# Copying the cache pages to DRAM ahead of time, and handing three kinds of low-part subtraction to GpSimd

## The chip, the cores and the metric

One NeuronCore of one Trainium2 chip runs the whole program. The metric is the device time of one execution in microseconds (us). A core has five engines with in-order instruction streams: TensorE (PE), VectorE (DVE), ScalarE (ACT), GpSimd (POOL) and SyncE (SP), which here issues nearly all DMAs.

## The reference

One inference step of a two-layer decoder trunk in float32, for one prompt of 1024 tokens and 8 sample rows of one token each, 1024 wide. Layer 0 is a Mamba-2 branch and a Conformer branch side by side. Layer 1 is sparse attention, and all that the change touches computes this:

```python
q, k, v, qi, ki, wi, z = odd_project(x, w_in)
scores = sum_h relu(qi_h . ki_all) * wi_h          # 8 index heads of 64
_, idx = lax.top_k(scores, 256)                    # per query
p = softmax(q . k_sel / 8)                         # 16 heads, 4 key heads
o = p . v_sel
y = layer_norm(ALPHA * x + (o * silu(z)) @ w_out)
```

For the 8 sample rows, keys, values and index keys of the past are read from paged caches: 8 rows times 8 pages of 128 positions, found through `page_table`. Prompt and sample rows share all weights.

## The kernel before

**Products in split float32.** A weight or activation is split into a high part (rounded to fp32r by a cast) and a low part (the difference), and a product is three matmuls, high x high, high x low, low x high (`mm3`, L132 to L134). `load_w` loads a 128x1024 block of weights in two halves of 128x512, casts each to its high part on ACT (L108) and subtracts to get the low part (L109) on DVE or POOL, by its argument `eng`. A projection block is one `load_w` and three column chunks (0, 344, 688) of 24 matmuls each.

**Layer 0** (about 0 to 937 us of the span) is a row of such blocks for the Conformer gate and values (GLU), the Mamba inputs, the gates and the output, with convolutions and recurrences on DVE and ACT beside them.

**Layer 1** has four parts that overlap.

- Index projections and index scores S (L970 to L977) and, for the sample rows, index keys read from the pages by 64 DMAs (`fetch`, L869; the page's number is loaded into a register of SP and used in the DMA's address), then scores Ss (L1006, L1024).
- Projections of queries (`QQ`, 8 blocks, L1045), keys (`KK`, 2 blocks) and gates (`ZZ`, 8 blocks). A query chunk leaves PSUM by a cast on ACT (L1051) and a subtraction from PSUM on DVE (L1052), and both parts go to DRAM. Sample keys are read from the pages by 64 more `fetch` DMAs and multiplied with the sample queries (L1104).
- The top-k of every row, a bitwise search for the threshold. Four blocks of query rows are searched together on DVE (search `d`, L1175: one counting pass per block and bit; 16 bits on the upper half word, 16 on the lower). Two blocks (search `a`) and the sample rows (search `s`) are searched by sign counts on ACT (L1164, tiles `jka` and `jks`), with three small DVE instructions per bit (L1166, L1148, L1150). Then masks are made on DVE (L1217 to L1245).
- Attention, 8 query tiles of 8 steps: logits (L1314), mask and maximum on DVE (L1315, L1318), exponentials on ACT (L1319), transposes (L1341), weighted values (L1350), and, between steps, the output product (L1402) and sample work, among it `sample_values`, which reads values by 64 `fetch` DMAs.

Python generators and a scheduler write the final order of each engine before the launch; at run time each engine goes through its own list in order and waits on semaphores. A tile tag with one buffer forces its uses into one sequence: a new tile of the tag comes after all uses of the tile before it. `jk` + name (L1163) gives each search a scratch tile of its own.

Of the kernel before, what the change touches and what calls it, by code (L numbers as in the profile page):

```python
# [124 lines left out]
def mm3(k, out, w, act, t0, n, m=128, halves=2, start=True, stop=True):  # L125

    nc = k.nc
    for kt in range(8):
# [5 lines left out]
        nc.tensor.matmul(out, wl, ah, start=False, stop=(stop and kt == 7))  # L134
# [42 lines left out]
def layer0(k):  # L177
# [232 lines left out]
    def xbc(i, dest):  # L410
# [290 lines left out]
    def out_b(m):  # L701
        w = load_w(k, A["W"][OB + m], eng=nc.gpsimd)
        for t0, n in CH:
# [114 lines left out]
def layer1(k):  # L818
# [35 lines left out]
    def ev(dt=F32):  # L854
        return k.t(tk, [128, 344], dt, "ev", 3)


    pgr = k.t(right, [1, 64], I32, "pgr")
    nc.sync.dma_start(pgr, A["pt"])

    def numbers(b, j, n):

        o = b * 8 + j
        return nc.values_load_multi_w_load_instructions(
            pgr[0:1, o : o + n], engines=[mybir.EngineType.SP],
            skip_runtime_bounds_check_because="a page table holds numbers of pages of the pool")[1]

    def fetch(dst, src, v, rows=128):
        nc.sync.dma_start(dst, src[bass.ds(v * rows, rows), :])  # L869
# [189 lines left out]
    for i in range(2):  # L1059
        w = load_w(k, A["W"][KK + i])  # L1060
# [57 lines left out]
    for i in range(8):  # L1118
        w = load_w(k, A["W"][ZZ + i])
# [13 lines left out]
    def search(name, R_, cols, count, above, last):  # L1133
# [582 lines left out]
```

## Time and profile before

| | us |
|---|---|
| median of 3 runs | 1729.22 (1726.86 to 1737.44) |
| profiled execution | 1731.68 |
| its span | 1729.9 |
| PE busy | 1607.1 (93%) |
| DVE busy | 1205.6 (70%) |
| ACT busy | 898.6 (52%) |
| POOL busy | 243.1 (14%) |

The profiled execution is 2.5 us above the median. The span leaves 1.8 us around it. Busy shares are means over the whole span; the stages have different limits, so the view by stretches is the one to read.

### The profile page before, as it was taken

The page shows a single profiled execution, that of the slowest core. Times are in us where ns is not written, and L with a number is a line of the kernel's source. Part 1 is how long each engine was busy: PE and PEld are TensorE (multiplying, and loading weights), DVE is VectorE, ACT ScalarE, POOL GpSimd, SP SyncE. Part 2 cuts the span into 40 slices and gives each one's busy share as a digit, 9 for nine tenths or more (in the row PEclk, how much of TensorE's full clock was granted, in tenths as well). Part 3 has the DMA queues.
Part 4 walks back from the last instruction along what each step waited for, and adds up shares of the span by engine and source line. Part 5 has one row for each costly group of instructions (what it writes and reads, how often), then busy time and mean ns, then how long its engine had stood idle before and what let it go on. Part 6 is the DMA issues. An engine that isn't in the chain of part 4 may idle for free.

```text
span 1729.9 us, 28861 instructions
## 1 busy us (share of the span) xinstructions
PE 1607.1 (93%) x10334; PEld 1443.8 (83%) x10334; DVE 1205.6 (70%) x2742; ACT 898.6 (52%) x2142; POOL 243.1 (14%) x280
## 2 busy tenths in 40 slices
PE   8988989998999998997998999598899899999996
PEld 7988989998999997996898998488889567676674
DVE  4778887426466878757665468999996766565673
ACT  5467464354345464535334455465752765555663
POOL 4000000001212234122322200000000411112120
PEclk9999999999999999998999999698999999999998
DMA  6222242246111145433421212242344723543460
GB/s 220 81 89 59 80 101 87 91 136 239 40 42 63 63 154 194 128 116 117 145 69 53 85 54 77 76 141 94 95 147 136 226 46 99 141 107 86 97 138 32
DMA packets 164497, 183.65 MB, mean 106 GB/s; under 512 B 20194, under 2 KB 131130, under 8 KB 164098
## 3 DMA queue, kind: packets, MB, share of 16 engines
q1 hardware_dynamic: 161842, 176.05, 34.2%
q0 software_dynamic: 1216, 4.37, 0.7%
q8 instruction: 81, 1.33, 0.3%
q10 hardware_dynamic: 1296, 1.38, 0.2%
q14 instruction: 62, 0.51, 0.1%
HBM read 129.81 MB, written 51.95 MB: 105 GB/s over the span
## 4 chain that ended last, share of the span: by engine, by line
PE 70%; DVE 20%; issue 3%; DMA 3%; ACT 2%; POOL 2%; DVEq 0%; ACTq 0%; POOLq 0%; SPq 0%
PE pp L132 12%; PE pp L134 12%; PE pp L133 12%; DVE jkd L1175 6%; PE po L1402 5%; PE pv L1350 4%; PE lg L1314 4%; PE tr L1341 4%; DVE uv L333 3%; PE pt L600 2%; PE pt L134 1%; PE pt L133 1%; PE pt L132 1%; PE pt L574 1%; PE po L1407 1%
## 5 line engine op out<-in xcount | busy, mean ns | idle before, releaser
L132 PE MATMUL pp<-act,whi 128*128 128x344 f32 x1088 | 353.7, 327 | 20.9 <-DVE uv L296 11.1
L134 PE MATMUL pp<-act,wlo 128*128 128x344 f32 x1088 | 354.6, 327 | 4.9 <-DVE wlo L109 4.9
L133 PE MATMUL pp<-act,whi 128*128 128x344 f32 x1088 | 353.5, 325 | 0.7 <-POOL act L699 0.7
L132 PEld LDWEIGHTS pp<-act,whi 128*128 128x128 f32 x1088 | 207.9, 192 | 24.7 <-DVE uv L296 11.6
L134 PEld LDWEIGHTS pp<-act,wlo 128*128 128x128 f32 x1088 | 208.1, 192 | 6.8 <-DVE wlo L109 5.1
L133 PEld LDWEIGHTS pp<-act,whi 128*128 128x128 f32 x1088 | 207.9, 191 | 3.1 <-issue 1.0
L108 ACT CAST whi<-wst 128x512 fp32r<-128x512 f32 x148 | 90.8, 618 | 146.2 <-PE pp L133 72.6
L333 DVE SCALAR_TENSOR_TENSOR uv<-uv,cst,uv 128x1024 f32<-128x1024 f32 x120 | 157.3, 1311 | 2.9
L132 PE MATMUL pp<-yh,whi 128*128 128x344 f32 x408 | 136.4, 334 | 16.4 <-DVE ev L1052 9.9
L109 DVE TENSOR_TENSOR wlo<-wst,whi 128x512 fp32r<-128x512 f32 x104 | 71.2, 690 | 106.5 <-ACT whi L108 106.4
L134 PE MATMUL pp<-yh,wlo 128*128 128x344 f32 x408 | 134.7, 330 | 3.3 <-DVE wlo L109 2.4
L1315 DVE CUSTOM_DVE_ANT_0 P<-lg,w 128x512 f32<-128x512 f32 (+3 forms) x144 | 83.0, 598 | 59.9 <-PE lg L1314 53.7
L348 ACT ACTIVATE cft<-cw,own 128x40 f32<-128x40 f32 x512 | 113.9, 313 | 13.2 <-DMA cw<-dct 8.6
L1314 PE MATMUL lg<-w,Q 128*128 128x512 f32 (+3 forms) x384 | 103.2, 372 | 2.3 <-DVE nmx L1315 2.0
L132 PEld LDWEIGHTS pp<-yh,whi 128*128 128x128 f32 x408 | 80.2, 197 | 21.2 <-DVE ev L1052 11.3
L1341 PE MATMUL tr<-cst,P 128*128 128x128 f32 x576 | 84.4, 279 | 3.2 <-ACT P L1319 2.1
L1341 PEld LDWEIGHTS tr<-cst,P 128*128 128x128 f32 x576 | 64.2, 141 | 26.2 <-issue 14.7
L1319 ACT ACTIVATE P<-P,mx 128x1024 f32<-128x1024 f32 (+3 forms) x64 | 63.3, 989 | 43.3 <-DVE mx L1318 42.7
L1350 PE MATMUL pv<-ph,V 128*64 128x256 f32 (+1 forms) x640 | 82.1, 372 | 2.4 <-DVE ph L1344 1.6
L134 PEld LDWEIGHTS pp<-yh,wlo 128*128 128x128 f32 x408 | 80.1, 196 | 4.7 <-DVE wlo L109 3.9
L109 POOL TENSOR_TENSOR wlo<-wst,whi 128x512 fp32r<-128x512 f32 x44 | 57.9, 1319 | 154.9 <-ACT whi L108 143.9
L1314 PEld LDWEIGHTS lg<-w,Q 128*128 128x128 f32 x384 | 62.5, 191 | 20.6 <-DVE nmx L1315 8.4
(567 smaller groups left out, 3850.8 us busy)
## 6 DMA issues: line engine op xcount, KB each, us to landing
wst<-in_W SPq DMA_DIRECT2D x148, 256.0 KB, 2.8
Q<-dq SPq DMA_DIRECT2D x64, 256.0 KB, 4.1
dq<-ev SPq DMA_DIRECT2D x48, 172.0 KB, 1.8
q<-in_ck SPq DMA_DIRECT2D x64, 128.0 KB, 2.4
vp<-in_cv SPq DMA_DIRECT2D x64, 128.0 KB, 2.2
xst<-in_xT SPq DMA_DIRECT2D x8, 516.0 KB, 9.0
dzb<-ob SPq DMA_DIRECT2D x24, 172.0 KB, 2.0
uv<-dzb SPq DMA_DIRECT2D x8, 516.0 KB, 5.0
```

Source lines behind the costliest of these rows:

```text
L108: nc.scalar.copy(hi, st)
L109: (eng or nc.vector).tensor_tensor(lo, st, hi.bitcast(F32), op=ALU.subtract)
L132: nc.tensor.matmul(out, wh, ah, start=(start and kt == 0), stop=False)
L133: nc.tensor.matmul(out, wh, al, start=False, stop=False)
L134: nc.tensor.matmul(out, wl, ah, start=False, stop=(stop and kt == 7))
L333: nc.vector.scalar_tensor_tensor(out, x, w[:, j : j + 1], y, op0=ALU.mult, op1=ALU.add)
L348: nc.scalar.activation(wv[:, :, ch, :], cw[:, g, : NBT - 1].rearrange("q (d p) -> q d p", p=PH), AF.Copy, scale=own[:, ch : ch + 1])
L1175: nc.vector.tensor_scalar(jk, col, c, 0.0, op0=op, op1=ALU.add, accum_out=cnt)
L1314: mm = nc.tensor.matmul(lg, Q[:, 4 * a + r, :], KT[g][:, s0 : s0 + m], start=(a == 0), stop=(a == 1))
L1341: nc.tensor.transpose(p[:, a, r * 128 : r * 128 + 128], Ps[r][:, (sb + a) * 128 : (sb + a) * 128 + 128], k.ident)
L1350: nc.tensor.matmul(pv[64 * u : 64 * u + 64, 256 * pr + c0 : 256 * pr + c1], V[:, sb + a, g * 64 : g * 64 + 64], ph[:, a, c0:c1], start=(sb ...
L1402: nc.tensor.matmul(p, a[:, kt, :], W[kt][w][:, sl], start=start and n == 0, stop=stop and n == 2, skip_group_check=True)
```

## The change

It does six things.

1. At the start of layer 0 it creates three DRAM buffers and copies all 192 cache pages into them in an order that later needs no page numbers (`four_pages`, four pages a call). Each call is written behind the middle column chunk of a projection block and wrapped in `tc.issue_after(mm)`. The later reads become plain DMAs: 8 for the index keys, 16 of 512 KB for the sample keys, 32 for the values.
2. A query chunk is read from PSUM twice by ACT (`hi` and `full`), and POOL makes `lo` from two SBUF tiles. The pool `ev` has 5 buffers, not 3.
3. The low parts of the query, key and gate weights (36 instructions of 128x512) go to POOL.
4. In search `d` one small DVE instruction per bit is folded into its neighbour.
5. Searches `a` and `s` share one scratch tile `jk` with one buffer.
6. The value tiles are pairs (`vp`, 6 buffers of two pages).

```diff
+    def four_pages(after):
+        if not todo:
+            return
+        what, b, hf = todo.pop(0)
+        with tc.issue_after(after):
+            o = b * 8 + 4 * hf
+            _, vs = nc.values_load_multi_w_load_instructions(
+                pgr[0:1, o : o + 4], engines=[mybir.EngineType.SP], ...)
+            for j, v in enumerate(vs, 4 * hf):
+                if what == "ckidx":
+                    nc.sync.dma_start(k.dki[j, b // 2, 64 * (b % 2) : 64 * (b % 2) + 64], A[what][bass.ds(v * 64, 64), :])
+                else:
+                    nc.sync.dma_start((k.dck if what == "ck" else k.dcv)[b, j], A[what][bass.ds(v * 128, 128), :])
...
-            mm3(k, p, w, x, t0, n)
+            mm = mm3(k, p, w, x, t0, n)
+            if t0 == 344:
+                four_pages(mm)
...
-        for b in range(NS):
-            for j, v in enumerate(numbers(b, 4 * hf, 4)):
-                fetch(kg[j // 2][64 * (b % 2) : 64 * (b % 2) + 64, j % 2, b // 2, :], A["ckidx"], v, 64)
+        for j in range(4):
+            nc.sync.dma_start(kg[j // 2][:, j % 2], k.dki[4 * hf + j].rearrange("r p x -> p r x"))
...
-        w = load_w(k, A["W"][QQ + i])
+        w = load_w(k, A["W"][QQ + i], eng=nc.gpsimd)
...
-            hi, lo = ev(F32R), ev(F32R)
+            hi, full = ev(F32R), ev()
             nc.scalar.copy(hi, p)
-            nc.vector.tensor_tensor(lo, p, hi.bitcast(F32), op=ALU.subtract)
+            nc.scalar.copy(full, p)
+            lo = ev(F32R)
+            nc.gpsimd.tensor_tensor(lo, full, hi.bitcast(F32), op=ALU.subtract)
...
+            flip = 1 << (bit - 1) if bit > last else 0
+            if bit < 31 and placed:
+                nc.vector.scalar_tensor_tensor(new, no, flip, cand, op0=ALU.bitwise_xor, op1=ALU.bitwise_xor)
...
-            jk = k.t(sc_pool, [128, 1032], BF16, "jk" + name, 1)[:rows, :w]
+            jk = k.t(sc_pool, [128, 1032], BF16, "jk", 1)[:rows, :w]
```

Where instructions stand now. On SP, in the first microseconds of layer 0, the order before was this (`wst` are weights, `xst` the input):

```order
L231 DMA xst_164<-in_xT 128x1032
L231 DMA xst_170<-in_xT 128x1032
L105 DMA wst_299<-in_W 128x512
L105 DMA wst_305<-in_W 128x512
L105 DMA wst_400<-in_W 128x512
L247 DMA dct_88<-taps_177 128x8x328
L105 DMA wst_406<-in_W 128x512
```

and in the changed kernel the same place reads (`pgr` is the page table, `dki` the index keys' buffer):

```order
L261 DMA xst_171<-in_xT 128x1032
L261 DMA xst_177<-in_xT 128x1032
L215 TENSOR_LOAD pgr_97
L220 ISA
L220 DMA dki_94<-in_ckidx 16x512
L220 ISA
L220 DMA dki_94<-in_ckidx 16x512
L220 ISA
L220 DMA dki_94<-in_ckidx 16x512
L220 ISA
L220 DMA dki_94<-in_ckidx 16x512
L105 DMA wst_319<-in_W 128x512
```

All 192 copies stand in this manner between the weight loads of the first seven GLU blocks; the last is SP's 487th row of 1057, just ahead of the first weights of the eighth block:

```order
L222 DMA dcv_15_96<-in_cv 16x2048
L222 ISA
L222 DMA dcv_15_96<-in_cv 16x2048
L105 DMA wst_2413<-in_W 128x512
```

On DVE, at the first attention instruction (L1315 before, L1350 now), the order before ended the sample rows' masks and a weight's low part first:

```order
L1241 TENSOR_SCALAR eq_14141<-Ss_9967,nxts_14135 8x1025
L1242 SCALAR_TENSOR_TENSOR cum_14142<-eq_14141 8x1025
L1243 SCALAR_TENSOR_TENSOR eq_14141<-cum_14142,needs_14139,eq_14141 8x1025
L1244 TENSOR_SCALAR cum_14142<-Ss_9967,nxts_14135 8x1025
L1245 TENSOR_TENSOR Ss_9967<-cum_14142,eq_14141 8x1025
L109 TENSOR_TENSOR wlo_12836<-wst_12833,whi_12835 128x512
L1315 ISA P_14194,nmx_14192<-lg_14195,w_12968 128x512
```

and now it is preceded by rounds of search `s` (`nos`, `cands`), 13 of them between the last mask of search `a` (the L1280 row) and the first L1350:

```order
L1280 TENSOR_TENSOR w_13254<-cum_14391,eq_14390 128x512
L1198 TENSOR_TENSOR nos_14119<-cnts_14118,lims_14066 8x1
L1180 SCALAR_TENSOR_TENSOR cands_14123<-nos_14119,cands_14115 8x1
...
L1198 TENSOR_TENSOR nos_14215<-cnts_14214,lims_14066 8x1
L1180 SCALAR_TENSOR_TENSOR cands_14219<-nos_14215,cands_14211 8x1
...
L1350 ISA P_14465,nmx_14463<-lg_14466,w_13253 128x512
L1350 ISA nmx_14463 128x1
```

Of the 32 rounds, 6 stand ahead of the end of search `a`'s masks, 13 here, and 13 between the attention steps of the first query tiles; the sample masks follow in steps 10 to 12, and the first output product follows 140 logit matmuls, where it followed 80 before. A piece of POOL's list now reads as follows in the last query blocks and the gates' weights; before, none of these rows stood on POOL:

```order
L109 TENSOR_TENSOR wlo_12195<-wst_12192,whi_12194 128x512
L1081 TENSOR_TENSOR ev_12074<-ev_12071,ev_12070 128x344
L109 TENSOR_TENSOR wlo_12201<-wst_12198,whi_12200 128x512
L109 TENSOR_TENSOR wlo_12341<-wst_12338,whi_12340 128x512
L109 TENSOR_TENSOR wlo_12347<-wst_12344,whi_12346 128x512
```

POOL keeps only these subtractions between the index scores and the first attention outputs.

## Rows read from the trace of the kernel before

**Rows 1.** The page's busy times, and its 40 slices of the span (one digit is the busy share in tenths).

```profile
PE 1607.1 (93%) x10334; PEld 1443.8 (83%) x10334; DVE 1205.6 (70%) x2742; ACT 898.6 (52%) x2142; POOL 243.1 (14%) x280
PE   8988989998999998997998999598899899999996
DVE  4778887426466878757665468999996766565673
PEclk9999999999999999998999999698999999999998
```

**Rows 2.** Busy time of each engine by stretch: start and end, length, then busy us (count) of PE, PEld, DVE, ACT, POOL, then the granted clock, DMA share and GB/s.

```profile
1060.00:1100.00 40.00, 32.69 (x170) 27.85 (x168) 38.35 (x101) 18.55 (x41) 0.84 (x2) 0.83 0.18 50
1100.00:1140.00 40.00, 24.89 (x120) 21.37 (x120) 38.95 (x123) 18.98 (x44) 0.00 (x0) 0.74 0.42 126
1140.00:1180.00 40.00, 33.34 (x175) 31.85 (x176) 39.56 (x131) 22.79 (x51) 0.00 (x0) 0.84 0.37 116
1180.00:1220.00 40.00, 37.12 (x221) 36.55 (x221) 39.34 (x136) 29.73 (x65) 0.00 (x0) 0.94 0.30 95
1220.00:1260.00 40.00, 35.07 (x251) 32.56 (x250) 39.28 (x133) 31.18 (x68) 0.00 (x0) 0.96 0.35 103
1260.00:1290.00 30.00, 26.51 (x214) 24.83 (x213) 29.56 (x87) 17.85 (x40) 0.00 (x0) 1.00 0.42 131
1290.00:1340.00 50.00, 49.89 (x408) 46.81 (x406) 36.43 (x65) 13.19 (x25) 0.00 (x0) 1.00 0.49 150
1340.00:1400.00 60.00, 54.59 (x345) 34.68 (x345) 46.18 (x122) 44.19 (x70) 23.25 (x14) 1.00 0.63 174
1400.00:1500.00 100.00, 99.47 (x706) 70.06 (x703) 62.12 (x198) 54.36 (x103) 10.29 (x14) 1.00 0.39 98
```

**Rows 3.** DVE in order of time around the end of the masks and the first attention instruction: start, length, line, operation, tiles, and in brackets the idle time before it with its releaser.

```profile
1314.79 0.69 DVE L109 TENSOR_TENSOR wlo<-wst,whi 128x512 fp32r<-128x512 f32 x1
1315.39 1.27 DVE L1217 TENSOR_SCALAR_CACHE_REDUCE eq<-Ss,cands 8x1025 bf16<-8x1025 f32 x1
...
1324.95 0.67 DVE L109 TENSOR_TENSOR wlo<-wst,whi 128x512 fp32r<-128x512 f32 x1
1338.03 0.69 DVE L1315 CUSTOM_DVE_ANT_0 P<-lg,w 128x512 f32<-128x512 f32 x1 [12.41 <-PE lg L1314]
```

**Rows 4.** SP's queue during the gather of the index keys, and PE's work in the same microseconds.

```profile
1059.92 49.37 SPq L869 DMA_DIRECT2D w<-in_ckidx  x64
1108.94 4.92 PE L1006 MATMUL pt<-w,q 128*64 128x128 f32 x26 [5.26 <-DMA w<-in_ckidx]
1121.05 0.65 PE L132 MATMUL pp<-yh,whi 128*128 128x344 f32 x1 [7.20 <-DVE ev L1052]
```

**Rows 5.** DVE between 1060 and 1345 us by line and shape: count, busy us and mean ns.

```profile
L109 DVE TENSOR_TENSOR wlo<-wst,whi 128x512 fp32r<-128x512 f32 x29 | 19.7, 679 | 0.1
L1052 DVE TENSOR_TENSOR ev<-pp,ev 128x344 fp32r<-128x344 f32 x18 | 9.1, 504 | 0.0
L1150 DVE TENSOR_SCALAR candd<-candd 128x4 uint32<-128x4 uint32 x15 | 2.5, 167 | 0.3
L1175 DVE TENSOR_SCALAR_CACHE_REDUCE jkd<-w,candd 128x1024 bf16<-128x1024 bf16 x15 | 19.1, 1276 | 0.3
L1166 DVE TENSOR_TENSOR nos<-cnts,lims 8x1 uint32<-8x1 f32 x32 | 4.5, 142 | 0.1
L1148 DVE SCALAR_TENSOR_TENSOR cands<-nos,cands 8x1 uint32<-8x1 uint32 x31 | 4.4, 143 | 0.0
L1150 DVE TENSOR_SCALAR cands<-cands 8x1 uint32<-8x1 uint32 x31 | 4.2, 136 | 0.0
```

**Rows 6.** ACT in the same stretch: the sign counts of search `s` with their reads, and the casts of query chunks.

```profile
L1164 ACT ACTIVATE jks<-Ss,cands 8x1025 bf16<-8x1025 f32 x32 | 36.9, 1152 | 26.8 <-DVE cands L1150 14.3 <-DVE canda L1148 10.1 <-DVE noa L1166 2.2
L1164 ACT ACTIVATION_READ_ACCUMULATOR jks<-Ss,cands 8x1 f32 x32 | 5.9, 185 | 0.0
L1051 ACT CAST ev<-pp 128x344 fp32r<-128x344 f32 x18 | 7.8, 431 | 3.9 <-PE pp L134 3.2 <-DMA dq<-ev 0.7
```

**Rows 7.** POOL over the whole span: low parts of weights; and of line 728, a subtraction of two SBUF tiles, least, median and longest ns on POOL.

```profile
L109 POOL TENSOR_TENSOR wlo<-wst,whi 128x512 fp32r<-128x512 f32 x44 | 57.9, 1319 | 154.9 <-ACT whi L108 143.9 <-issue 6.7 <-ACT E L606 3.7
L728 POOL TENSOR_TENSOR yb<-ya,yh x6: 909/1196/5206, 810.0 to 841.6; 128x344 fp32r<-128x344 f32 x6
```

**Rows 8.** POOL and DVE side by side in attention, then line 1318 over the whole span (least, median, longest ns), an instruction on 128x1 elements with two SBUF inputs.

```profile
1348.13 4.73 POOL L1394 TENSOR_TENSOR wl<-z,wh 128x1024 fp32r<-128x1024 f32 x2 [268.98 <-DVE mx L1318]
1350.56 0.66 DVE L1315 CUSTOM_DVE_ANT_0 P<-lg,w 128x512 f32<-128x512 f32 x1
1351.14 1.74 DVE L1318 TENSOR_TENSOR mx<-nmx 128x1 f32<-128x1 f32 x1
1352.80 1.21 DVE L1344 COPY ph<-tr 128x1024 f32<-128x1024 f32 x1
L1318 DVE TENSOR_TENSOR mx<-nmx x64: 128/159/1737, 1339.5 to 1559.1; 128x1 f32<-128x1 f32 x64
L1318 DVE TENSOR_TENSOR mx<-nmx 128x1 f32<-128x1 f32 x63 | 15.4, 245 | 1.2
```

**Rows 9.** ACT in the first 60 us of attention, by line and shape.

```profile
L1319 ACT ACTIVATE P<-P,mx 128x1024 f32<-128x1024 f32 x16 | 18.4, 1149 | 10.1 <-DVE mx L1318 10.1
```

**Rows 10.** Line 869, the page reads, on SP: least, median and longest ns of an issue; SP in order of time in a run of sample key reads; and the first weight loads on SP.

```profile
L869 SPq DMA_DIRECT2D w<-in_ckidx x64: 468/468/1316, 1059.9 to 1108.8; - x64
L869 SPq DMA_DIRECT2D q<-in_ck x64: 332/333/1244, 1121.9 to 1326.4; - x64
1291.31 4.06 SPq L869 DMA_DIRECT2D q<-in_ck  x7
22.25 2.99 SPq L105 DMA_DIRECT2D wst<-in_W  x3
38.17 18.76 SPq L105 DMA_DIRECT2D wst<-in_W  x5
0.00:100.00 100.00, 86.54 (x548) 85.25 (x548) 65.23 (x71) 57.72 (x189) 20.45 (x47) 1.00 0.40 131
100.00:200.00 100.00, 94.91 (x592) 94.34 (x593) 78.14 (x91) 53.28 (x203) 0.25 (x2) 0.94 0.31 93
```

**Rows 11.** The output product of the first attention outputs on PE, first and last start.

```profile
L1402 PE MATMUL po<-wh,yh x112: 387/394/480, 1402.3 to 1704.3; 128*128 128x512 f32 x112
```

More of the change, by code (lines that the diff above doesn't have):

```diff
@@ L133, in mm3 @@
         nc.tensor.matmul(out, wh, al, start=False, stop=False)
-        nc.tensor.matmul(out, wl, ah, start=False, stop=(stop and kt == 7))
+        last = nc.tensor.matmul(out, wl, ah, start=False, stop=(stop and kt == 7))
+    return last.ins
 def load_stacked(k, src, m):
@@ L193, in layer0 @@
     tmp = es.enter_context(k.pool("tmp0"))
+    pages = ctx.enter_context(tc.tile_pool(name="pages", bufs=1, space=DRAM))
+    k.dki = k.t(pages, [8, 4, 128, 128], F32, "dki")
+    k.dck = k.t(pages, [8, 8, 128, 256], F32, "dck")
+    k.dcv = k.t(pages, [8, 8, 128, 256], F32, "dcv1")
+    pgr = k.t(tmp, [1, 64], I32, "pgr")
+    nc.sync.dma_start(pgr, A["pt"])
+    todo = [("ckidx", b, hf) for hf in range(2) for b in range(NS)]
+    todo += [("ck", b, i % 2) for i in range(8) for b in (i // 2, i // 2 + 4)]
+    todo += [("cv", b, hf) for f in range(2) for hf in range(2) for b in range(4 * f, 4 * f + 4)]
+    def four_pages(after):
[5 more added lines that the diff above has]
+            _, vs = nc.values_load_multi_w_load_instructions(
+                pgr[0:1, o : o + 4], engines=[mybir.EngineType.SP],
+                skip_runtime_bounds_check_because="a page table holds numbers of pages of the pool")
+            for j, v in enumerate(vs, 4 * hf):
[3 more added lines that the diff above has]
+                    nc.sync.dma_start((k.dck if what == "ck" else k.dcv)[b, j], A[what][bass.ds(v * 128, 128), :])
     big = lambda: k.t(obp, [128, T + 30], F32, "big", 3)
@@ L854, in ev @@
     def ev(dt=F32):
[L855 to L869, printed above, removed]
+        return k.t(tk, [128, 344], dt, "ev", 5)
     KIH, KIL = ra(tag="ki"), ra(tag="ki")
@@ L1097, in sample_keys @@
         for n, b in enumerate(bs):
-            for j, v in enumerate(numbers(b, i % 2 * 4, 4)):
-                fetch(kp[n][:, j, :], A["ck"], v)
+            nc.sync.dma_start(kp[n], k.dck[b, i % 2 * 4 : i % 2 * 4 + 4].rearrange("j p x -> p j x"))
         for j in range(4):
@@ L1128, in layer1, with search @@
         nc.scalar.copy(SL[:, hf * 512 : hf * 512 + 512], lg[hf])
-    def search(name, R_, cols, count, above, last):
+    def search(name, R_, cols, count, above, last, placed=False):
         n = len(cols)
@@ L1175, in count, with above @@
             nc.vector.tensor_scalar(jk, col, c, 0.0, op0=op, op1=ALU.add, accum_out=cnt)
-        cand = search(name, 128, UP, count, lambda no, cnt: nc.vector.tensor_scalar(no, cnt, float(TOPK), None, op0=ALU.is_lt), 16)
+        def above(no, cnt, bit):
+            nc.vector.tensor_scalar(no, cnt, float(TOPK), float(1 << bit) if bit < 31 else 1.0, op0=ALU.is_lt, op1=ALU.mult)
+        cand = search(name, 128, UP, count, above, 16, placed=True)
         top = sm("top", U32)
@@ L1514, in sample_values @@
         for b in range(4 * f, 4 * f + 4):
-            for j, v in enumerate(numbers(b, 2 * jp, 2), 2 * jp):
-                vps[j, b] = k.t(lt, [128, 256], F32, "vp", 12)
-                fetch(vps[j, b], A["cv"], v)
+            vp = k.t(lt, [128, 2, 256], F32, "vp", 6)
+            nc.sync.dma_start(vp, k.dcv[b, 2 * jp : 2 * jp + 2].rearrange("j p x -> p j x"))
+            for j in range(2):
+                vps[2 * jp + j, b] = vp[:, j, :]
         yield
```

41 lines of the change are left out of this document (26 added, 15 removed).

## The prediction

> **What bounds the kernel now.** I read the page first, then the busy time by stretch, and then time-ordered rows at the seams between stages. The page [rows 1] shows PE at 93% and DVE at 70%, but its slices of 43 us tell more: DVE stands at 9 in the 26th to 30th (1081 to 1297 us), and in the 26th PE falls to 5 tenths and its clock to 6. The stretches give the numbers [rows 2]. From 1060 to 1290 us DVE is busy for 225 of 230 us: here the bitwise search bounds the kernel. PE meanwhile loses 7.3 + 15.1 + 6.7 + 2.9 + 4.9 + 3.5 = 40.4 us of idle time, and its granted clock falls to 0.74 to 0.96, between the levels of 1.2 and 2.4 GHz. From 1290 to 1340 PE is full, and in attention (1400 to 1500) it is full again with 99.5 of 100 us. The seam is visible on DVE [rows 3]: the masks of search a end at 1315.4, those of the sample rows at about 1325, and then DVE waits 12.4 us for logits, since PE still works off what it lost. Attention begins at 1338.0. So a saved microsecond of DVE counts until PE is the later one, and what attention gets handed over decides the rest.
>
> A part of PE's loss is not DVE's. The 64 index-key reads hold SP's queue for 49.37 us, and PE waits 5.26 us for them and soon after 7.20 us for a query chunk, whose transfers stand behind them on SP [rows 4].
>
> **Layer 1, what DVE sheds.** Up to the end of the masks of search a, 28 weight low parts (0.679 us), 18 query subtractions (9.1 us), 15 folded instructions (2.5 us) and 26 rounds of search s at 0.142 + 0.143 + 0.136 us leave DVE [rows 5]: 19.0 + 9.1 + 2.5 + 10.9 = 41.5 us by durations. Neighbours overlap: the 0.69 us low part at 1314.79 is followed after 0.60 us [rows 3]. By that ratio of 0.87 it is 36 us, and the masks of a would end at 1315.4 - 36 = 1279.
>
> **What DVE gets back as a wait.** The shed work goes to POOL, which is idle in this stretch: 28 x 1.319 us and 18 x 0.909 to 1.196 us [rows 7], about 55 us in some 210, a share of 26%. It is not free for DVE. In attention a maximum over 128x1 elements, two SBUF inputs, took 1.74 us when it began inside a 4.73 us pair of POOL subtractions, and 0.159 at the median; the masking instruction just before it, one input from PSUM, took its usual 0.66 [rows 8]. So a DVE instruction with two SBUF inputs stands still until the running POOL instruction ends. The mean over all 63 is 245 ns, 86 above the median [rows 8], at a POOL share of 33.5/160 = 21% in the first 160 us of attention [rows 2]. At 26% that is about 110 ns for each. The search has many such instructions: two per round of search a (64), one per upper bit of d (15), two per lower bit (32), two in each of six rounds of s (12), about ten in the masks, together 133. That is 15 us. The counting passes (one input) are not touched. I bound this wait by 5 us (few meet) and 30 us (POOL's queries and weights come in bursts while the chain of small instructions passes). The Trainium skill says the same of the mechanism, in "SBUF — State Buffer", section "SBUF: two separate sides": the port pair that DVE and GpSimd share is an exclusive lock for a whole instruction, and a DVE instruction needs it if it has two SBUF inputs or runs in a two-port mode. By half a POOL instruction of waiting at each meeting it would be an estimated 21 us and not 15, and the sum would stand 6 us higher. So the masks of a end at about 1279 + 15 = 1294.
>
> **Search s now comes last.** With one shared `jk` tile its rounds can only follow those of a. In the order 13 rounds stand between the masks of a and the first attention instruction. A round is a chain: 1.152 + 0.185 us on ACT [rows 6] and 0.42 us on DVE [rows 5], 1.76 us, about 1.9 with the hand-overs, at most 2.3 if other work comes between. 13 x 1.9 = 25 us. The first mask of attention would start at 1294 + 25 = 1319 in place of 1338.0: **-19 us**, between 1279 + 5 + 23 = 1307 (-31) and 1279 + 30 + 30 = 1339 (+1). PE can follow: from 1060 to 1338 it idled 40.5 us, of which SP's 12.5 us certainly go, and DVE's part shrinks with DVE. ACT's second copy of each query chunk is 24 x 0.431 = 10 us [rows 6], covered since ACT is busy for 19 to 31 us of each 40 [rows 2]; without that cover it would cost those 10 us.
>
> **Attention pays.** The other 13 rounds of s run among its first steps. ACT is busy for 44.19 of 60 us there [rows 2], mostly with exponentials at 1.149 us [rows 9]; 13 x 1.34 = 17.4 us more makes 61.6, over the full 60, and DVE waits in order for each count. I take 5 us, between 2 and 8. The sample masks, 1315.39 to 1324.95 in [rows 3], 9.6 us of DVE, move into steps 10 to 12, where DVE is busy 62% [rows 2]: in 18 us it would have 11 + 9.6, so 4 us, between 2 and 6. The output product, first at 1402.3 [rows 11], follows 60 logit matmuls later, 7.5 steps in which PE lacks that filler. PE idled 5.4 us in the first 60 us of attention without it [rows 2], some 0.55 per step of 6 us; 7.5 steps make 4 us, between 1 and 6. Together **+13 us**, 5 to 20.
>
> **Layer 0 pays a little.** `issue_after` names a matmul, an instruction of PE; the copies are SP's, and the order shows them tied to nothing: all stand among the weight loads of the first seven GLU blocks and are not spread over the layer. These blocks are 7 x 144 = 1008 matmuls; at 548 in the first and 592 in the second 100 us [rows 10] that is 178 us. SP loads weights there in a loose rhythm [rows 10] and has room: a page read cost it 0.77 us in the gather with its page numbers (49.37/64, [rows 4]) and 4.06/7 = 0.58 in a steady run of sample keys [rows 10], so 192 copies are 111 to 148 us, and 28 weight issues at 0.4 add 11. Weights would come 3 to 5 us late at worst, and they are loaded a block ahead. The copies add some 19 MB to the 22 MB of the first 200 us, at a DMA share of 0.40 and 0.31 [rows 10]; twice that is still under full. A copy from DRAM to DRAM is not in this trace; the near rows are these reads. I take **+2 us**, nearest the steady run, between 0 and, if a copy holds SP for 1.0 us, 192 + 11 - 178 = 25 us. The later reads become fewer and larger; PE's 12.5 us behind SP are counted above, and in attention no row shows a wait for SP, so 0.
>
> **Sum.** -19 + 13 + 2 = -4 us: the profiled 1731.7 becomes 1727.7. It stood 2.5 above the median, so on the scale of the runs **1725 us**.
>
> **Rivals.** (1) *The trade comes off.* POOL's instructions seldom meet the small ones and the rounds of s hide behind PE, which is the later engine anyway: -31 + 5 + 0 = -26, 1703 us. For it speaks that DVE is the bound for 230 us; against, that 133 instructions have to slip through a POOL busy for a quarter of the time. (2) *Slower through the search's tail.* The small instructions meet POOL often (30 us), so the masks of a end at 1309 and attention starts no earlier than before, and then still carries 13 rounds, the sample masks and the late output product at their upper price: +1 + 20 + 2 = +23, 1752 us. It decides once DVE loses over 30 us to POOL, that is 225 ns per small instruction. If even counting passes had to wait for POOL, DVE would lose all 55 us. The clause on two-port modes in the section of the Trainium skill named above would do that to them only if they ran in such a mode. Against that, a counting pass over 128x1024 2-byte elements took 1.276 us [rows 5], and a float32 one over 8x1025 took 1.27 [rows 3]. (3) *SP falls behind.* A copy DRAM to DRAM costs SP 1.0 us or more; GLU weights come up to 25 us late and PE starves in the first 200 us: -4 - 2 + 25 = +19, 1748 us. It decides above 167/192 = 0.87 us per copy. (4) *The change does not do what it says:* the copies are not placed behind matmuls. The order shows that this is so; it is in the forecast, with no price unless (3) holds.
>
> **Chances.** Forecast 0.45, (1) 0.27, (2) 0.15, (3) 0.13. What a measurement can tell from no change is about 1%, 17 us. Forecast's own range is 1712 to 1738. Case (1) and a low tail of the forecast are faster: 0.30. Case (2) and (3) in good part slower: 0.23. The rest, 0.47, is within 1%. The range takes in (1) nearly whole and the middle of (2) and (3): 1700 to 1749.
>
> **What would show it.** In the changed profile: the DVE low parts gone between 1060 and 1300 and POOL busy for 60 us or more there; small DVE instructions with two SBUF inputs at means well above 0.16 us; the last mask of a near 1294, the first attention mask near 1319 (both shifted by what layer 0 costs); sign counts of s between exponentials; the first output product some 45 us after the first mask more than before; no wait of PE for GLU weights in the first 178 us. A first attention mask before 1305 would speak for (1), one after 1335 for (2); PE waits on weight loads early for (3). I am wrong altogether if attention's pace itself changes.

## The result: slower by 1.5%

The changed kernel takes 1755.97 us at the median (1754.86 to 1756.68, 4 runs) against 1728.47 beside it: a ratio of 1.0148 (95% interval 1.0124 to 1.0172). I forecast 1725 us, in a range of 1700 to 1749, so the time lies outside it, on the side that I gave 0.23.

The profiled execution has a span of 1754.8 us against 1729.9, 24.9 more. Five marks in the two traces divide it. The first three count PE's matmuls, whose order in layer 0 hardly changed; the 6400th is not the same instruction in the two kernels, but from the 5900th to the 6300th the lateness stands at 20.5 to 20.6 us, so its mark can be used.

| start of | before | changed | late by | my term |
|---|---|---|---|---|
| the 1400th matmul (layer 0) | 245.7 | 265.2 | 19.5 | |
| the 4400th matmul (layer 0) | 722.4 | 739.1 | 16.7 | +2 |
| the 6400th matmul (index scores) | 1065.2 | 1085.7 | 20.5 | 0 |
| the first attention mask | 1338.0 | 1350.7 | 12.7 | -19 |
| the end | 1729.9 | 1754.8 | 24.9 | +13 |

Layer 0 cost 16.7 us and not 2; the start of layer 1 another 3.8; the search gave back 7.8 and not 19; attention cost 12.2 (391.9 us from its first mask to the end before, 404.1 now), near the 13 of the forecast.

**Layer 0.** Busy time by stretch in the changed kernel, to be set beside [rows 10]:

```profile
0.00:100.00 100.00, 85.90 (x540) 83.94 (x541) 59.93 (x68) 53.30 (x168) 15.32 (x47) 1.00 0.58 179
100.00:200.00 100.00, 80.60 (x478) 79.28 (x478) 64.82 (x73) 54.50 (x217) 0.25 (x2) 0.86 0.70 208
```

The loss is between 100 and 200 us: 478 matmuls in place of 592, PE idle for 19 us and its granted clock at 0.86. SP's queue there, then ACT, then PE's wait, in the same trace (`SPq` and `ACTq` are DMA issues on these engines):

```profile
95.13 20.81 SPq L222 DMA_DIRECT2D dck<-in_ck  x27
116.04 0.53 SPq L342 DMA_DIRECT2D out_cfconv_s<-us  x1
...
118.00 0.53 SPq L375 DMA_DIRECT2D cw<-dct  x1
```

```profile
118.37 0.33 ACTq L324 DMA_DIRECT2D us<-in_cfctx  x1
118.75 2.95 ACT L384 ACTIVATE cft<-cw,own 128x40 f32<-128x40 f32 x13 [7.43 <-DMA out_cfconv_s<-us]
...
PE pp L132 <- ACT big L313: 9.7, 2, 5.3
```

The reader sees 27 copies in one run at 0.77 us each, a small store behind them, and ACT standing for 7.43 us because its own list holds a DMA issue (L324) that waits for a completion from SP's queue. The sigmoid that frees PE's accumulator is queued behind that issue, and PE waits 5.3 us for it. Twice this happens; the kernel before has no wait of PE for line 313's counterpart in these 100 us. After the first matmul, all waits of PE over 0.6 us in the first 215 us sum to 24.2 us, 9.4 before; the stretches at a granted clock of one half sum to 27.3 us there, 13.7 before. SP issued the weight loads late (12.8 us later than before at 92 us, 21.2 at 196), but a load landed 2.7 to 4.1 us after its issue between 20 and 200 us, and PE's waits for a weight's cast sum to 0.3 us in the first 210.

**The search.** GpSimd's new work, and the small comparisons on DVE, in the changed kernel (1040 to 1352 us):

```profile
L109 POOL TENSOR_TENSOR wlo<-wst,whi 128x512 fp32r<-128x512 f32 x35 | 48.1, 1381 | 160.6 <-ACT whi L108 160.6
L1081 POOL TENSOR_TENSOR ev<-ev,ev 128x344 fp32r<-128x344 f32 x24 | 23.7, 987 | 74.4 <-ACT ev L1079 58.6 <-issue 15.8
...
L1198 DVE TENSOR_TENSOR noa<-cnta,lima 128x2 uint32<-128x2 f32 x32 | 12.4, 388 | 0.1
L1180 DVE SCALAR_TENSOR_TENSOR canda<-noa,canda 128x2 uint32<-128x2 uint32 x31 | 7.3, 236 | 0.0
```

`noa` took 147 ns before and `canda` 150. Both read two SBUF tiles, and both now wait for running GpSimd instructions. One such meeting, GpSimd's instruction and then DVE's:

```profile
1228.42 1.27 POOL L109 TENSOR_TENSOR wlo<-wst,whi 128x512 fp32r<-128x512 f32 x1 [7.95 <-ACT whi L108]
1228.64 1.06 DVE L1198 TENSOR_TENSOR noa<-cnta,lima 128x2 uint32<-128x2 f32 x1
```

Of search a's 95 small instructions 24 began while a GpSimd instruction ran. Their mean is 582 ns and that of the other 71 is 158; 21 of the 24 ended 15 to 25 ns after the end of the GpSimd instruction. One of the 21 has a single input (393 ns); the rest have two. Counted from each DVE instruction's start to the next one's, from the first comparison of search d to the end of search a's last mask, the time divides so (us; S is the sum that makes the index scores):

| | all | weight lows | query lows | a, small | s, small | d, small | S | counting passes |
|---|---|---|---|---|---|---|---|---|
| before | 245.2 | 17.0 | 8.3 | 8.6 | 8.9 | 11.9 | 11.2 | 121.2 |
| changed | 234.9 | 0 | 1.0 | 20.5 | 4.4 | 13.3 | 12.4 | 123.0 |

Then come the 13 rounds of search s, about 1.87 us each, of which DVE waits 1.37 us for one count on ACT:

```profile
1326.03 1.68 DVE L1280 TENSOR_TENSOR w<-cum,eq 128x512 bf16<-128x512 f32 x1
...
1329.50 0.15 DVE L1198 TENSOR_TENSOR nos<-cnts,lims 8x1 uint32<-8x1 f32 x1 [1.37 <-ACT jk L1196]
...
1350.29 0.15 DVE L1198 TENSOR_TENSOR nos<-cnts,lims 8x1 uint32<-8x1 f32 x1 [1.37 <-ACT jk L1196]
...
1350.73 0.67 DVE L1350 CUSTOM_DVE_ANT_0 P<-lg,w 128x512 f32<-128x512 f32 x1
```

PE came to this seam hardly sooner than DVE: its first attention logits start at 1348.5 us, 2.2 before the mask (at 1337.3 in the kernel before, where DVE waited for them [rows 3]). With PE as late as it was, an earlier end of the search would have gained at most these 2.2 us.

**Attention.** Its output product now starts 116.6 us after the first mask and not 64.3 [rows 3, 11], and PE's idle time from the first mask to the end is 21.0 us and not 10.9:

```profile
L1437 PE MATMUL po<-wh,yh x112: 387/394/496, 1467.3 to 1729.5; 128*128 128x512 f32 x112
```

### The profile page after: what moved, and what is told of

The parts are those of the page before. It is cut to its first block, busy times and chain, and to the rows that moved or that the text cites. A ratio compares the mean times of both kernels' runs of the same rounds, so it can differ in the third digit from the quotient of the medians.

```text
span 1754.8 us, 28858 instructions
## 1 busy us (share of the span) xinstructions
PE 1613.5 (92%) x10334; PEld 1444.5 (82%) x10334; DVE 1194.7 (68%) x2668; ACT 904.4 (52%) x2166; POOL 310.3 (18%) x340
## 4 chain that ended last, share of the span: by engine, by line
PE 62%; DVE 20%; issue 5%; DMA 4%; ACT 4%; SPq 4%; POOL 1%; ACTq 0%; DVEq 0%; POOLq 0%
PE pp L132 10%; PE pp L134 10%; PE pp L133 10%; DVE jkd L1207 7%; PE po L1437 4%; PE pv L1385 4%; PE tr L1376 3%; PE lg L1349 3%; DVE uv L369 3%; SPq L222 2%; PE pt L638 2%; DVE S L1005 1%; SPq L220 1%; PE pt L134 1%; PE pt L132 1%
## 5 line engine op out<-in xcount | busy, mean ns | idle before, releaser
L132 PE MATMUL pp<-act,whi 128*128 128x344 f32 x1088 | 355.5, 328 | 35.6 <-ACT big L313 13.6
L132 PEld LDWEIGHTS pp<-act,whi 128*128 128x128 f32 x1088 | 209.0, 193 | 40.2 <-ACT big L313 14.7
L109 POOL TENSOR_TENSOR wlo<-wst,whi 128x512 fp32r<-128x512 f32 x80 | 107.5, 1348 | 362.0 <-ACT whi L108 351.0
L109 DVE TENSOR_TENSOR wlo<-wst,whi 128x512 fp32r<-128x512 f32 x68 | 46.5, 691 | 120.1 <-ACT whi L108 118.1
L384 ACT ACTIVATE cft<-cw,own 128x40 f32<-128x40 f32 x512 | 114.3, 315 | 21.8 <-DMA out_cfconv_s<-us 12.7
L1350 DVE CUSTOM_DVE_ANT_0 P<-lg,w 128x512 f32<-128x512 f32 (+3 forms) x144 | 82.9, 596 | 51.5 <-PE lg L1349 46.4
L1196 ACT ACTIVATE jk<-S,canda 128x640 bf16<-128x640 f32 x64 | 49.7, 776 | 77.6 <-DVE canda L1182 73.4
L1349 PEld LDWEIGHTS lg<-w,Q 128*128 128x128 f32 x384 | 63.1, 191 | 26.0 <-DVE nmx L1350 12.7
```

Source lines behind the costliest of these rows:

```text
L109: (eng or nc.vector).tensor_tensor(lo, st, hi.bitcast(F32), op=ALU.subtract)
L132: nc.tensor.matmul(out, wh, ah, start=(start and kt == 0), stop=False)
L384: nc.scalar.activation(wv[:, :, ch, :], cw[:, g, : NBT - 1].rearrange("q (d p) -> q d p", p=PH), AF.Copy, scale=own[:, ch : ch + 1])
L1349: mm = nc.tensor.matmul(lg, Q[:, 4 * a + r, :], KT[g][:, s0 : s0 + m], start=(a == 0), stop=(a == 1))
L1350: nc.vector.tensor_tensor_reduce(out=P[:, s0 : s0 + m], in0=lg, in1=M[tb][:, s0 : s0 + m], scale=-0.125, scalar=BIG, op0=ALU.add, op1=ALU. ...
```

## The experiments

Twelve kernels ran. All ratios are against the kernel before on the same chip; the chips differ, so medians of runs of different chips are compared with care: the kernel before took 1728.47 us beside the changed one, 1728.77 beside e1 to e4, 1730.45 beside e5 to e8, 1728.77 beside e9 to e11 and 1730.48 beside e12. "4400th" is the start of that matmul, "logits" the start of PE's first attention logits, "tail" the time from the first attention mask to the end of the profiled span.

| run | median us | ratio (95%) | 4400th | logits | first mask | tail |
| --- | --- | --- | --- | --- | --- | --- |
| before | 1728.47 | 1 | 722.4 | 1337.3 | 1338.0 | 391.9 |
| changed | 1755.97 | 1.0148 (1.0124 to 1.0172) | 739.1 | 1348.5 | 1350.7 | 404.1 |
| e1 | 1751.54 | 1.0130 (1.0113 to 1.0147) | 719.3 | 1345.5 | 1346.6 | 404.0 |
| e2 | 1761.47 | one run | 739.3 | 1359.1 | 1360.2 | 399.4 |
| e3 | 1790.47 | one run | 758.5 | 1384.2 | 1386.0 | 402.6 |
| e4 | 1726.11 | 0.9986 (0.9974 to 0.9997) | 718.7 | 1320.1 | 1322.4 | 401.9 |
| e5 | 1713.32 | 0.9912 (0.9896 to 0.9929) | 717.8 | 1316.9 | 1317.7 | 391.2 |
| e6 | 1713.02 | 0.9899 (0.9883 to 0.9916) | 715.5 | 1299.7 | 1303.4 | 409.1 |
| e7 | 1705.37 | 0.9853 (0.9837 to 0.9870) | 718.2 | 1303.7 | 1308.5 | 396.3 |
| e8 | 1714.46 | 0.9915 (0.9898 to 0.9931) | 717.3 | 1320.3 | 1321.1 | 391.2 |
| e9 | 1707.55 | 0.9886 (0.9865 to 0.9907) | 718.2 | 1308.6 | 1313.3 | 392.3 |
| e10 | 1706.28 | 0.9879 (0.9860 to 0.9898) | 715.7 | 1307.0 | 1310.9 | 391.8 |
| e11 | 1730.64 | 1.0019 (1.0007 to 1.0030) | 736.4 | 1325.0 | 1329.8 | 397.0 |
| e12 | 1754.72 | 1.0138 (1.0121 to 1.0155) | 736.2 | 1344.8 | 1347.3 | 405.4 |

**What layer 0 pays for.** e1 takes the copies out:

```diff
-    def four_pages(after):
-        ...
+    def four_pages(after):
+        pass
...
-            nc.sync.dma_start(kp[n], k.dck[b, i % 2 * 4 : i % 2 * 4 + 4].rearrange("j p x -> p j x"))
+            for j, v in enumerate(numbers(b, i % 2 * 4, 4)):
+                fetch(kp[n][:, j, :], A["ck"], v)
...
```

> The changed kernel with its page copies undone (pages read by 64 + 64 + 64 DMAs in layer 1, as before); all else as changed. Theory A (the copies cost layer 0 its time, whatever else is true): the 4400th PE matmul starts at 722 us as before and not at 739, layer 0 gives back 17 us; layer 1 loses again what the copies saved there (PE waits of about 12 us behind SP's gather near 1100 us, of which some is covered), so the total is 1739 to 1750 us. Rival B (layer 0 is slower for another reason, say the code's placement): the 4400th matmul stays near 739.

Measured: 719.3, so all of layer 0's loss belongs to the copies. The total of 1751.5 lies 1.5 us above my range: it fell by only 4.4 us. What the copies cost in layer 0 they seem to give back in layer 1, but e1 does not price that cleanly. SP's gather is back and PE waits 6.1 us for the index keys; but the planner also put 21 rounds of search s, not 13, between the last mask of a (its end at 1305.6, 1327.7 in the changed kernel) and the first attention mask:

```profile
1304.92 0.69 DVE L1273 TENSOR_TENSOR w<-cum,eq 128x512 bf16<-128x512 f32 x1
...
1346.18 0.15 DVE L1191 TENSOR_TENSOR nos<-cnts,lims 8x1 uint32<-8x1 f32 x1 [2.54 <-ACT jk L1189]
...
1346.61 0.67 DVE L1343 CUSTOM_DVE_ANT_0 P<-lg,w 128x512 f32<-128x512 f32 x1
```

That stretch takes 41.0 us and not 23.0, and PE is as late there (first logits at 1345.5). So the 1.3% by which e1 is slower than the kernel before is the price of the rest of the change in this order, and not of its parts. e2 and e3 ask what it is about the copies.

```diff
 e2, added to e1 (the index keys likewise, 4 rows of 64):
...
+                    nc.sync.dma_start((k.dck if what == "ck" else k.dcv)[b, j, 0:8], A[what][bass.ds(v * 128, 8), :])
...
 e3, added to e1, 24 times and on every second call (the index keys as 256 KB):
...
+                nc.sync.dma_start((k.dck if what == "ck" else k.dcv)[b].rearrange("j p x -> (j p) x"), A[what][b * 1024 : b * 1024 + 1024, :])
```

> As e1, plus 192 copies in layer 0 with the same page numbers and issues on SP at the same places, but of one sixteenth of the bytes, into buffers nobody reads (what layer 1 needs is read as in e1). Theory A1 (SP's queue: 192 issues hold up the other DMAs behind them): layer 0 is as late as in the changed kernel, the 4400th matmul at 735 to 741 us. Rival A2 (DMA traffic of 19 MB more): at 722 to 726 us, near e1.

> As e1, plus 24 large copies in layer 0 (256 KB or 1 MB each, contiguous, DRAM to DRAM, no page numbers) of the same 18.9 MB into buffers nobody reads. Theory A1 (SP's queue): the 4400th matmul at 722 to 726 us. Rival A2 (traffic): at 735 us or later.

Busy time by stretch of e2 (100 to 200 us), of e3 (0 to 100 us):

```profile
100.00:200.00 100.00, 83.37 (x481) 82.05 (x482) 65.90 (x75) 55.74 (x222) 0.25 (x2) 0.86 0.28 78
```

```profile
0.00:100.00 100.00, 57.70 (x338) 56.73 (x339) 28.90 (x41) 34.40 (x91) 18.44 (x47) 0.83 0.89 302
```

e2 loses the same as the changed kernel, 739.3 against 739.1, with a DMA share of 0.28 and not 0.70: the issues on SP are enough to explain the loss, the bytes are not needed. e3 missed my expectation of 722 to 726 by far. Its 24 issues took 23.5 us of SP and not 99.2 as the 192 copies' own issues do, but all of them went out in the first 100 us, at a DMA share of 0.89; one of them held SP for 11.6 us, two weight loads issued at 41 and 46 us landed 24.0 and 19.8 us later, and PE stood once for 34 us:

```profile
PE pp L132 <- ACT whi L108: 34.0, 1, 34.0
```

So traffic is not harmless either when it comes in a block. e4 keeps the bytes and the issues and changes the place:

```diff
-                four_pages(mm)
+                four_pages(k.last_load.ins)      # in all six places; last_load is load_half's DMA on SP
```

> The changed kernel with each group of four copies ordered behind its own block's weight load on SP (an instruction of the same queue) and not behind a matmul; all else as changed. Theory A1: SP is no longer full, the copies spread over 48 blocks, layer 0 gives back at least 12 of its 17 us: 4400th matmul at 722 to 727 us, total 1738 to 1744 us. Rival A2: the same bytes at any time cost the same, 4400th matmul near 739 and total near 1756 us.

```profile
0.00:100.00 100.00, 86.65 (x548) 85.63 (x548) 65.07 (x71) 57.66 (x186) 12.90 (x47) 1.00 0.45 142
100.00:200.00 100.00, 94.24 (x596) 93.13 (x597) 79.24 (x91) 53.66 (x205) 0.25 (x2) 0.97 0.35 102
```

Layer 0 runs a little sooner than before, 718.7, and the total fell by 30 us to 1726.1, better than my 1738 to 1744. 20.4 us of the gain are there by the 4400th matmul and 27.7 by the 6400th; where the 7.3 between them come from no run takes apart. e11 repeats the test on the best kernel below, in the other direction.

> e7 with the page copies where the change has them (behind nothing, among the first seven blocks' weights). Theory A1: layer 0 is late again by about 20 us (the 4400th matmul near 738 against 718), total 1722 to 1728, so that the placement of the copies alone turns e7's gain into no change. Rival: the 20 us are partly covered by the faster layer 1: under 1718.

1730.6 against e7's 1705.4: the placement alone is worth some 25 to 29 us there (27 when each is set against the kernel before on its chip, 29 by the ratios). The time lies 3 us above my upper bound.

e12 asks for the chain by which a full SP stops PE:

```diff
-        nc.sync.dma_start(A["cfconv_s"][i], s[:, 1:31, :])
+        nc.gpsimd.dma_start(A["cfconv_s"][i], s[:, 1:31, :])
```

> The changed kernel with the eight small stores of the new convolution context (out_cfconv_s, 30 KB per 128x240 tile) issued by GpSimd and not by SP; the copies stay where they are. Theory C (PE's long waits in layer 0 come by this chain: a store waits on SP behind 27 copies, ACT's DMA issue waits for its buffer, ACT's band tiles and sigmoid wait behind that issue, and PE for the sigmoid): the two waits of PE for ACT's sigmoid near 114 to 131 and 185 to 190 us (9.7 us) shrink to under 3, the 4400th matmul falls from 739 to 725 to 733 us, total 1742 to 1751. Rival C0 (another transfer behind the copies, the coefficients cw or the dcu, dcv round trips, is as late): 4400th matmul at 736 or later.

It gave 736.2, rival C0's side, and 1754.7 in all, above my range. PE's two waits for the sigmoid stayed (9.9 us, 9.7 in the changed kernel), and so did ACT's, with another name at its end:

```profile
116.67 0.34 ACTq L324 DMA_DIRECT2D us<-in_cfctx  x1
117.05 2.30 ACT L384 ACTIVATE cft<-cw,own 128x40 f32<-128x40 f32 x10 [5.43 <-DMA dck<-in_ck]
```

The waits written into ACT's list explain it. That issue stands as follows in the changed kernel and in e12:

```
L324 DMA us_1466<-in_cfctx 128x240 [waits DMAHW2_49,DMAHW6_49,DMAHW0_49,DVE_49]
L324 DMA us_1466<-in_cfctx 128x240 [waits DMAHW6_49,DMAHW7_49,DMASW3_49,DVE_49]
```

The store became a GpSimd completion (DMASW3). The counter DMAHW6 stands in both lists: it is the one that this issue of ACT's raises itself when it lands, and the eight such counters are shared by SP's and ACT's DMAs in turn. In the written order the last DMA that raises DMAHW6 to the awaited value is a page copy on SP, the 104th of the 192 in the changed kernel and the 106th in e12. So in both kernels ACT waits for a page copy, and in the changed one for the store behind it as well (the copy lands at 115.7 us, the store at 118.2). What is shown is the order and the wait; no run took the sharing away, so what PE would gain without it stays open.

**What the shared tile and GpSimd pay.** e4 to e7 are the four combinations of the two, all with spread copies. They differ also in the buffers of `ev` (5 in e4 and e6, 4 in e5, 3 in e7) and in the order that the planner makes of each.

```diff
 e5, own scratch tiles:
-            jk = k.t(sc_pool, [128, 1032], BF16, "jk", 1)[:rows, :w]
+            jk = k.t(sc_pool, [128, 1032 if name == "s" else 640], BF16, "jk" + name, 1)[:rows, :w]
-        return k.t(tk, [128, 344], dt, "ev", 5)
+        return k.t(tk, [128, 344], dt, "ev", 4)
 e6, low parts on DVE:
-        w = load_w(k, A["W"][QQ + i], eng=nc.gpsimd)
+        w = load_w(k, A["W"][QQ + i])                 # also KK and ZZ
...
-            nc.gpsimd.tensor_tensor(lo, full, hi.bitcast(F32), op=ALU.subtract)
+            nc.vector.tensor_tensor(lo, p, hi.bitcast(F32), op=ALU.subtract)
 e7: both, ev with 3 buffers
```

> e4 (copies spread) with a scratch tile of its own for each sign search (jk of search a 640 wide, and ev with 4 buffers and not 5, to make room). Theory J (the shared tile is what slows attention): the first attention mask to the end falls from 402 us in e4 to 391 to 395 as in the kernel before, ACT no longer stands for search a with weight casts queued behind it, and the total is 1710 to 1720 us. Rival J0 (attention is slower for the copied pages or for something else): still 400 to 403 us, total 1724 or more.

1713.3, and the tail falls from 401.9 to 391.2: theory J holds. With low parts on DVE the same step (e6 to e7) takes the tail from 409.1 to 396.3, and the total from 1713.0 to 1705.4.

The traces show one more price of the shared tile, at the start of layer 1. Between the 5700th and the 5900th matmul every kernel with the shared tile (changed, e1 to e4, e6, e12) falls back by 2.6 to 4.5 us against the kernel before, and no kernel with tiles of its own does (e5, e7 to e11: 0.0). With the shared tile some 192 matmuls of lines 937 to 939 or their counterparts (tile `pt`) stand there in a row, where with tiles of their own 28 others come after the first 112; and in that row PE waits once, here in the changed kernel:

```profile
974.63 0.39 PE L937 MATMUL pt<-w,yh 128*128 128x264 f32 x1 [2.25 <-DVE wi L943]
```

> e4 with the three kinds of low parts back on DVE (weights, and queries from PSUM); the scratch tile stays shared. Theory L (DVE sheds some 36 us and gets back about 15 as waits for running GpSimd instructions): the small comparisons of search a (noa) fall from a mean of 388 ns to about 147, the last of them comes at 1290 to 1300 us and not 1275, total 1735 to 1748 us. Rival L1 (the waits eat all that was shed): last noa near 1275, total within 3 us of e4's 1726. Rival L2 (the waits cost nothing): last noa at 1308 or later.

Here I was wrong: 1713.0, some 13 to 15 us faster than e4 and far under my 1735, and the last `noa` came at 1266.3 us, 8.8 sooner than in e4 and not 15 to 25 later. `noa` did return to its old price:

```profile
L1196 DVE TENSOR_TENSOR noa<-cnta,lima 128x2 uint32<-128x2 f32 x32 | 5.0, 155 | 0.0
```

and DVE's time from the first comparison to the last mask of a rose by only 6.7 us, from 234.3 to 241.0, since the waits went as the work came. But the planner also put 2 rounds of search s between that mask and the first attention mask, where e4 has 13, and that wait shrank from 23.1 us to 3.0. This pair therefore mixes two things. e5 and e7, where all rounds of s come earlier, are the better pair:

> e4 with both undone: own scratch tiles, all low parts on DVE, ev with 3 buffers; what is left of the change are the copied pages (spread) and the folded instruction of search d. Expected: as the kernel before, less a part of the 12.5 us that PE waited behind SP's gather and 2.5 us of folding: 1716 to 1726 us, first mask to end at 391 to 394 us. If pages alone give nothing: 1728.

1705.4, the best of all and 11 us under my range's lower end; its tail of 396.3 us lies above my 391 to 394, and five of the seven larger mask instructions of the sample rows stand behind its first attention mask, where e5 has all seven ahead. DVE's stretch is 242.9 us in e5 and 242.8 in e7: GpSimd's subtractions took nothing off DVE, for waits of the small instructions and of DVE for ACT ate it all (`noa` has a mean of 194 ns in e5, with the same subtractions on GpSimd as in e4, where it is 388: how many meet is a matter of the order). On PE it cost time: the first logits start at 1316.9 us in e5 and at 1303.7 in e7. ACT in e5 (first three rows), PE in e5, and the stretch 1180 to 1260 us of e5 and of e7:

```profile
1246.30 0.43 ACT L1152 ACTIVATE ev<-pp 128x344 f32<-128x344 f32 x1
1248.38 1.15 ACT L1196 ACTIVATE jks<-Ss,cands 8x1025 bf16<-8x1025 f32 x1 [1.65 <-DVE cands L1182]
...
1250.34 0.60 ACT L108 CAST whi<-wst 128x512 fp32r<-128x512 f32 x1
...
1250.99 0.65 PE L132 MATMUL pp<-yh,whi 128*128 128x344 f32 x1 [4.60 <-ACT whi L108]
...
1180.00:1260.00 80.00, 66.66 (x433) 62.97 (x432) 78.33 (x266) 57.20 (x126) 12.77 (x10) 0.87 0.33 108
```

```profile
1180.00:1260.00 80.00, 70.04 (x496) 65.14 (x495) 78.81 (x277) 58.61 (x127) 0.00 (x0) 0.94 0.38 120
```

A weight's cast is queued on ACT behind counts that wait for DVE's search; PE stands for 4.6 us, and its next 5.0 us run at half the clock. By the lengths of the matmuls such stretches sum to 40.4 us between 1060 and 1330 in e5 and to 17.5 in e7; the granted clock itself is at one half for 44.4 and 27.3 us there. PE's waits for weight casts between 1060 and 1330 us sum to 14.9 us in e5 and 3.7 in e7. e8, e9 and e10 ask which of GpSimd's pieces does it.

```diff
 e8: e5 with the query subtraction back on DVE
 e9: e5 with load_w(k, A["W"][QQ + i]), and so for KK and ZZ
 e10: e7 with load_w(k, A["W"][ZZ + i], eng=nc.gpsimd)
```

> e5 with the query subtraction back on DVE from PSUM (ev with 3 buffers); GpSimd keeps the 36 weight low parts. By theory L GpSimd is then busy for 48 us and not 72 in the search, noa's mean falls from 388 ns to some 300, and DVE pays 24 x 0.43 = 10 us: within 6 us of e5 in either direction, 1708 to 1724 us.

> e5 (copies spread, own scratch tiles, ev with 4 buffers) with the 36 weight low parts back on DVE; GpSimd keeps only the 24 query subtractions. e5 and e8 lost 8 to 9 us to e7 and both have the weights on GpSimd. Theory W (the weights do it: their casts come late on ACT, PE waits 2 to 5 us for them and then runs a stretch at the lower clock): PE's half-clock stretches between 1060 and 1330 us sum to 20 us or less (e7 17.5, e5 40.4), total 1702 to 1708. Rival W0 (any GpSimd work in the search costs it, through the waits of DVE): 1709 or more.

> e7 (copies spread, own scratch tiles, low parts on DVE) with only the 16 low parts of the gate weights on GpSimd. Theory W: PE waits for weight casts in the gate blocks, the half-clock stretches grow from 17.5 to 22 us or more, total 1707 to 1713. Rival W1 (gate weights come when the search is nearly over, and DVE sheds 10 us): 1697 to 1704.

e8 gave 1714.5, like e5 (`noa` at 251 ns, not some 300). e9 gave 1707.6 with 19.8 us at half the clock, inside theory W's range. But e9 ran on another chip than e5, e7 and e8; set against the kernel before on its own, e9 is 21.2 us faster, between e5's 17.1 and e7's 25.1, and W0's 1709 is within the difference of the chips. So the total does not decide between W and W0. PE's own time speaks for W. From 1060 us to the first logits:

| | e7 | e10 | e9 | e5 | e8 |
|---|---|---|---|---|---|
| PE idle, us | 24.5 | 27.7 | 29.0 | 28.9 | 35.6 |
| granted clock at one half, us | 17.1 | 23.9 | 20.5 | 44.4 | 30.7 |
| first logits | 1303.7 | 1307.0 | 1308.6 | 1316.9 | 1320.3 |

The two kernels with all 36 weight low parts on GpSimd come to attention 13 to 17 us later than e7, the one with the query subtractions alone 5. The way is not always the weight's cast: in e8 the waits for casts sum to 5.5 us, and 10.1 are for ACT copies out of PSUM (`qs`) that stand behind the counts in the same manner. In total time the weights cost some 4 to 9 us (e5 against e9, e8 against e7), since the longer tail of e7 takes a part back; what the query subtractions cost lies between nothing (e5 against e8) and 4 us (e9 against e7). e10 settled less: 1706.3 lies between the two ranges and its 20.4 us between e7's and my threshold; against the kernel before it is 2.6 us behind e7, and its logits start 3.3 us later. That the 20 query and key weights are the dear ones follows by elimination and was not run alone.

## Why the prediction was wrong, point by point

The profiled span was forecast to fall by 4 us and rose by 24.9. Of these 28.9 us, layer 0 makes 14.7, the start of layer 1 3.8, and the search with its seam 11.2; attention gives back 0.8.

- **Layer 0, +2 us: the step that failed most.** It measured 16.7. I wrote that weights "would come 3 to 5 us late at worst". The pace was 0.77 us per copy in long runs, the upper end of my own bounds and under the 0.87 at which rival (3) was to decide. Two things were missing from the sum. I counted copies and weight issues against 178 us, but SP also carries the convolution's stores and round trips, 27 other issues in the first 200 us beside 28 weight loads, and a weight issue took 0.53 us there where I had 0.4: 192 x 0.77 + 55 x 0.53 = 177 us, so by this estimate no room was left; weight loads were 13 us late at 92 us and 21 at 196. And I asked only whether weights come late. PE's long waits came through ACT, whose list holds a DMA issue that waits for SP. Rival (3) named the right queue, with the wrong threshold and the wrong way to PE.
- **DVE's relief, -36 + 15.** By the table about 33 us were shed (17.0 and 7.3 of low parts, some 7 of rounds of s, some 2 of folded instructions), and since the last mask of a came only 10.3 us sooner after the search began, not 21, about 22 were paid. The mechanism was right: instructions with two SBUF inputs waited, and search a's small ones alone paid 11.9 us. The size was off on both sides, most on what was paid. The Trainium skill ("SBUF — State Buffer", section "SBUF: two separate sides") calls the port pair that DVE and GpSimd share an exclusive lock for a whole instruction. The trace agrees: 21 of 24 such instructions ended 15 to 25 ns after GpSimd's; and the 22 paid lie nearer to the estimate of 21 that I worked out for it than to my 15.
- **Search s, +25 us.** 13 rounds of 1.87 us, 23.0 us from the last mask of a to the first attention mask. Right.
- **PE as cover.** I let PE follow wherever DVE led. In the changed kernel its first logits start at 1348.5 us, 2.2 before the mask, so it would have held a faster search back; in e5 DVE waited 2.24 us for them. The waits for weight casts and other ACT work, and the lower clock after them, made PE as late as DVE or later.
- **Attention, +13 us.** Measured 12.2; e4 to e5 shows that the shared tile is its cause. How the 12.2 divide among the counts on ACT, the sample masks and the late output product was not measured, so that the three estimates add up so well may be luck.
- **The start of layer 1** was late by another 3.8 us, for which I had nothing. It goes with the shared tile: the seven kernels that have it lose 2.6 to 4.5 us there, the six others nothing. Why the planner's order differs there stays open.
- **The copied pages themselves** I priced only where PE had waited for SP before. Well placed and without the rest (e7, which also has the folded instruction of search d), they bring 25 us, 1.5%. Between 1060 us and the first logits PE's idle time falls from 40.4 to 24.5 us and its time at half the clock from 54.6 to 17.1, far more than the 12.5 us of waits behind SP that I had.

## What to carry to other kernels

Before moving DMAs to an earlier stage, add up everything that their queue already carries there, and look for engines whose own lists hold an issue or a wait on that queue: an order tied to an instruction of another engine is no order on the queue. Work that goes to an idle engine is not free when the busy engine's instructions stand while it runs, or when its inputs are queued behind waits. A scratch tile shared by two chains puts one behind the other, and the price can appear in other stages: here in attention and at the start of layer 1.

## What the runs showed of the hardware

- A DVE instruction of two elements per partition with two SBUF inputs took a mean of 388 ns beside 72 us of GpSimd subtractions in the changed kernel and 147 to 155 without them; in e5, with the same subtractions in another order, it took 194. The mean is made by the few that began while GpSimd ran and ended with it. Counting passes with one input stayed at 1.28 us for 1024 elements [rows 5].
- In the changed kernel's trace 20 stops of PE after the first matmul were longer than 2 us; beside 17 of them stands a stretch of 3 to 14 us at a granted clock of one half, and three (at 48.7, 666.6 and 1184.7 us) have none. In e5 a wait of 4.6 us was followed by 5.0 us at half the clock.
- A page copy DRAM to DRAM of 128 KB and one of 8 KB cost SP the same: 27 in a row took 20.81 us in the changed kernel and 20.82 in e2, and layer 0 was as late.
- 19 MB of large copies issued together (e3) started the 4400th matmul 39 us later than no copies (e1); the same bytes in page copies spread over 48 blocks (e4) did not make it later.
